# A two-layer hybrid trunk on one core: weights stored as contiguous load blocks, places of their own for the opening's loads and for the norm's outputs

## The chip, the cores and the metric

One core of one Trainium2 chip. The metric is the device time of one execution in microseconds (us). Engines go by the profile's names: PE (matmul), PEld (weight load, overlaps PE), DVE, ACT, POOL, and SP, whose queue issues most of the DMAs (SPq in rows).

## The reference, cut to what matters

512 tokens (256 context, then 256 latent) of width 1024 go through two layers; only the latent half is returned.

```python
for l in range(2):
    mod  = ada_w[l].T @ silu(c) + ada_b[l]         # six vectors of 1024, for two conditionings
    h    = x * (1 + mod.scale) + mod.shift
    p    = h @ w_in[l]                             # one projection for four mixers
    y    = concat(gdn(p), s5(p), hgrn(p), retention(p)) @ w_out[l]
    x    = layer_norm(alpha * x + mod.gate * y)
    h    = x * (1 + mod.scale2) + mod.shift2
    y    = swiglu(h, ffn_w1, ffn_w3, ffn_w2) if l == 0 else top2_of_8_experts(h, moe_w1, moe_w3, moe_w2)
    x    = layer_norm(alpha * x + mod.gate2 * y)
```

## The kernel before, in words

Activations lie feature-major: 128 features on the partitions, 512 tokens in the free dimension, eight such tiles (`KT`). A product in f32 accuracy is made of three passes in f32r: `weight` (L338) loads a raw tile by a DMA on SP's queue (L344), ACT copies it to a rounded `whi` (L348), DVE subtracts to get `wlo` (L263), and PE runs `whi` on `xh`, `whi` on `xl` and `wlo` on `xh` (L331). Most weight tiles are 512 KB (128x1024 f32) in three raw buffers `wraw`; the mixture of experts has tiles of 1 MB (128x2048) in eight buffers `mraw` (L1756).

All weights but the conditioning lie in DRAM as in the reference. A tile of `w_in`, `w_out` of layer 0 or the dense feed-forward is a strided cut: 128 rows per k-tile of 128 columns, so pieces of 512 bytes (1024 bytes where 256 columns are taken). For `moe_w1` and `moe_w3` the pieces are 2048 bytes; for `moe_w2`, `w_out` of layer 1, `ada_w` and the input `xt` a partition's piece is one whole row, 2 or 4 KB.

The order of the work (`run`, L2032):

1. `setup`, then in the pool `start` the modulation of layer 0, parts 0 and 1 (`ada`, L392): 8 loads of 512 KB each (L399) into the tag `sraw`, which has **12 buffers**, used raw by PE against the conditioning (`csk`).
2. `first_input` (L417): four 512 KB loads of `xt` (L426) into the same tag `sraw`; DVE (context half) and ACT (latent half) apply scale `sc1p` and shift, and write `xh` and `xl`.
3. `mixers(0)`: projections from `w_in`, S5 tables built on DVE and POOL (loads `s5B`, `s5C`, L1263; transposes on PE, L1278; a round trip through DRAM, `s5wt` to `s5w`), and the four mixers with their scans. A scan's input goes through DRAM too (`s5u`).
4. `mixed` (w_out, residual), `norm_feat` (L1488) with `keep` = a store of `x` to `xt1` on ACT's queue (L2045).
5. S5 tables of layer 1, `ada(1, 0)`, `ada(1, 1)`, the dense `ffn`, `ada(1, 4)`, `ada(1, 5)`, `norm_feat` again; its `keep` transposes `x` on PE (L2067), copies the result to a second tile `t` on ACT and stores `t` to `xtok` on ACT's queue (L2069).
6. `mixers(1)`, `mixed_tok` (loads `lres` from `xtok`), the mixture of experts (8 experts x 7 chunks x 6 loads of 1 MB) and the last norm.

`norm_feat`'s `m` (the modulated tile that becomes `xh`, `xl`), its `x` and the `t` of `keep` all come from `s2()` (L232): three shared buffers, in the profile `k2A`, which the mixers and the feed-forward use as well. A new tile waits until the readers of the tile three before it are done, a store among them.

The order of the instructions on each engine and each queue is fixed when the kernel is built: a list scheduler runs a model of the kernel's dependences, buffers and durations, with offsets on some functions (`prior`), and every engine and queue then works strictly in the order that it gave. A buffer more, or a load whose modelled duration changes, can therefore move instructions on every engine.

Of the kernel before, what the change touches and what calls it, by code (L numbers as in the profile page):

```python
# [143 lines left out]

def input_arrays(x):
# [14 lines left out]
    for k in ("ada_w", "w_in", "w_out", "ln_g", "ln_b", "ffn_w1", "ffn_w3", "ffn_w2", "moe_w1", "moe_w3", "moe_w2"):  # L160
        arrays[k] = np.ascontiguousarray(g(k))
# [27 lines left out]
class Trunk:  # L189
# [148 lines left out]
    def weight(self, src, shape, hi_eng="act", lo_eng="vec", pool=None, raw_bufs=3, bufs=2, tag="w", raw=None):  # L338
# [52 lines left out]
    def ada(self, l, part, pool=None, tag="w", bufs=3):  # L391
# [25 lines left out]
    def first_input(self, pool, bufs):  # L417
# [6 lines left out]
        for k0 in range(0, KT, 2):  # L424
            raw = self.t("sraw", [2, NTOK], F32, bufs, pool)
# [30 lines left out]
    def product(self, w, xh, xl, n, fn):  # L456

        for i in range(w.shape[2] // P):
            acc = self.ps("acc")[:, :n]
            self.stationary(w[:, :, i * P:(i + 1) * P], xh, xl, acc)  # L460
# [3 lines left out]
    def proj_feat(self, l, c0, fn, tok=(0, NTOK), ncol=256):  # L464

        w = self.A["w_in"][l].rearrange("(k p) f -> p k f", p=P)[:, :, c0:c0 + ncol]
        a, b = tok
        self.product(w, self.xh[:, :, a:b], self.xl[:, :, a:b], b - a, fn)

    @projecting  # L470
    def proj_tok(self, l, c0, fn, blocks, ncol=256):

        w = self.A["w_in"][l].rearrange("(k p) f -> p k f", p=P)[:, :, c0:c0 + ncol]
        blocks = list(blocks)
        accs = [self.ps("acc") for _ in range(0, len(blocks), 2)]
        for k0 in range(0, KT, 4):
            hi, lo = self.weight(w[:, k0:k0 + 4], [4, ncol], "act", "vec")
# [12 lines left out]
    def proj_few(self, l, c0, m, dst):  # L490

        w = self.A["w_in"][l].rearrange("(k p) f -> p k f", p=P)[:, :, c0:c0 + m]
        hi, lo = self.weight(w, [KT, m])
# [396 lines left out]
    def gdn_proj(self, l, full):  # L890
# [11 lines left out]
        self.proj_few(l, C_GAB, 16, self.gab)  # L902
# [586 lines left out]
    def norm_feat(self, r, pm, l, sub, part, l2, keep):  # L1489
# [28 lines left out]
        for k in range(KT):  # L1518
            x = self.s2()
# [51 lines left out]
    def mixed(self, l, src):  # L1571
# [4 lines left out]
        w = self.A["w_out"][l].rearrange("(k p) f -> p k f", p=P)  # L1576
# [13 lines left out]
    def out_part(self, l, ks, last=None):  # L1590
        w = self.A["w_out"][l].rearrange("(k p) f -> p k f", p=P)
        for k in ks:
            hi, lo = self.weight(w[:, k], [D])
# [28 lines left out]
    def ffn(self, l, xt, r):  # L1622
        A = self.A
        NF = FF // P
        w1, w3, w2 = (A[k][0].rearrange("(k p) f -> p k f", p=P) for k in ("ffn_w1", "ffn_w3", "ffn_w2"))
        gs = [[self.t(f"fg{c}{j}", [NF // 2, NTOK], F32R) for c in "hl"] for j in range(2)]
        gh, gl = ([gs[f // (NF // 2)][c][:, f % (NF // 2)] for f in range(NF)] for c in range(2))
        for f in range(NF):
            h = self.s2()
            sl = slice(f * P, f * P + P)  # L1630
            self.product(w1[:, :, sl], self.xh, self.xl, NTOK, lambda i, acc: self.silu(h, acc, self.s2()))
            self.product(w3[:, :, sl], self.xh, self.xl, NTOK, lambda i, acc: self.mul(h, h, acc))
# [120 lines left out]
    def raw_unit(self, src, n):  # L1753

        raw = self.t("mraw", [2048], F32, self.RAW, self.open["mr"][1])
        self.nc.sync.dma_start(raw.rearrange("p (a b) -> p a b", a=n), src)  # L1756
        return raw

    def unit(self, src, n, lo="vec"):
        raw = self.ahead.pop(0) if self.ahead else self.raw_unit(src, n)  # L1760
        return self.weight(src, [n, 2048 // n], "act", lo, self.mw, bufs=3, tag="m", raw=raw)

    def up_srcs(self, w1, w3, c):

        return [w[:, k0:k0 + 4, c * 512:c * 512 + 512] for w in (w1, w3) for k0 in range(0, KT, 4)]

    def up_parts(self, w1, w3, c, start=0):
        for src in self.up_srcs(w1, w3, c)[start:]:
            yield self.unit(src, 4)

    def expert(self, e):
        return [self.A[k][0].rearrange("e (k p) f -> p e k f", p=P)[:, e] for k in ("moe_w1", "moe_w3", "moe_w2")]

    def load_ahead(self):

        srcs = [src for c in range(2) for src in self.up_srcs(*self.expert(0)[:2], c)]
        self.ahead = [self.raw_unit(src, 4) for src in srcs[:self.RAW]]
# [21 lines left out]
    def down(self, w2, y, g, c):  # L1799
# [8 lines left out]
        for j0 in range(0, 4, 2):  # L1808
            hi, lo = self.unit(w2[:, 4 * c + j0:4 * c + j0 + 2, :], 2)
# [42 lines left out]
    def experts(self, jobs, first=False):  # L1852
# [5 lines left out]
        early = [self.unit(src, 4, "pool") for src in self.up_srcs(*jobs[0][:2], 0)[:3]]  # L1858
        parts = self.up_parts(*jobs[0][:2], 0, 3)
        self.ex, self.exi = [None, None], 0  # L1860
        x = {0: self.gather(jobs[0][3])}
        y, g, back = {}, {}, None
        for i in range(len(steps) + 1):
            if i < len(steps):
                n, c = steps[i]
                if i > 0:
                    parts = self.up_parts(*jobs[n][:2], c)
                g[i] = self.up(chain(early if i == 0 else (), parts), x[n])
                if c == NC - 3 and n + 1 < len(jobs):
                    x[n + 1] = self.gather(jobs[n + 1][3])  # L1870
# [5 lines left out]
            if i > 0:  # L1876
# [3 lines left out]
                self.down(jobs[n][2], y[n], g.pop(i - 1), c)  # L1880
                if c == NC - 1:
                    back = self.scatter(x[n], y[n], jobs[n][4]())
        back()

    def moe(self, l, ns):
# [17 lines left out]
        for j in range(2):  # L1903
# [8 lines left out]
        self.experts([self.expert(e) + [[self.pos[:, j, e:e + 1] for j in range(2)],  # L1912
                                               lambda e=e: [self.rG[:, j, e:e + 1] for j in range(2)]]
                      for e in range(NE)], True)
        n = nc.values_load(self.nover[0:1, 0:1], min_val=0, max_val=3)
        with self.tc.For_i(0, n, 1) as it:  # L1916
# [5 lines left out]
            dyn = [A[k][0][ds(e, 1)].rearrange("e (k p) f -> p (e k) f", p=P) for k in ("moe_w1", "moe_w3", "moe_w2")]  # L1922
# [178 lines left out]
```

## Time and profile before

| | before |
|---|---|
| three runs | 2549.09, 2555.69, 2555.76 us (median 2555.69) |
| profiled execution | 2555.49 us, its span 2553.7 us |
| PE busy | 2287.9 us, 90% |
| PEld / DVE / ACT / POOL busy | 70% / 68% / 50% / 21% |
| moved by DMA | 532.76 MB, mean 209 GB/s |
| packets under 2 KB | 169457 of 338197 |

The span runs from the first to the last instruction of the profiled execution; 1.79 us of its time lie around it. A row of a timeline gives start, duration, engine, line, operation, output<-input, and in brackets the idle time before it with what ended it. PEclk is the granted clock of PE as a share of 2.4 GHz.

### The profile page before, as it was taken

Reading aid. Unit: us, or ns where it says so; the run is one execution under the profiler, and the core shown is the slowest. Engines: PE = TensorE matmul, PEld = TensorE weight load, DVE = VectorE, ACT = ScalarE, POOL = GpSimd, SP = SyncE. Lnnn points to the kernel's source line nnn. Section 1 sums busy time; section 2 is a strip of 40 time slices with the busy share of each in tenths; the row PEclk is TensorE's granted clock in tenths of the full one; section 3 lists DMA queues with packets and bytes.
Section 4 is the critical chain, followed back from the end, with each engine's and each line's share of the span. In section 5 each row is a group of like instructions: output and inputs, shape, how many; then the busy total and the mean of one; then the engine's idle time right before and its main releaser. Section 6 shows DMA issues by size and latency. Waiting matters only on the chain. (4 is left out here: it accounts for less than half of the span.)

```text
span 2553.7 us, 33393 instructions
## 1 busy us (share of the span) xinstructions
PE 2287.9 (90%) x12928; PEld 1790.7 (70%) x12928; DVE 1737.5 (68%) x2352; ACT 1273.1 (50%) x1475; POOL 532.4 (21%) x490
## 2 busy tenths in 40 slices
PE   4979988878899999878896859999999999999997
PEld 1767756554788887447675648878787878788885
DVE  8645636778533322445646689888888888889887
ACT  1542523422544422353533337767676767676774
POOL 4423433327322200333323140000000000001000
PEclk7889987879999999888987869999999999999998
DMA  8343252415533333653230449989898989899994
GB/s 282 115 145 95 80 164 68 153 48 199 153 99 99 97 124 101 213 169 93 64 117 26 146 140 352 371 308 370 308 370 314 363 312 373 316 368 334 370 358 167
DMA packets 338197, 532.76 MB, mean 209 GB/s; under 512 B 32497, under 2 KB 169457, under 8 KB 337649
## 3 DMA queue, kind: packets, MB, share of 16 engines
q1 hardware_dynamic: 312304, 512.79, 58.4%
q10 hardware_dynamic: 25728, 17.77, 2.4%
q8 instruction: 104, 1.70, 0.3%
q14 instruction: 61, 0.49, 0.1%
HBM read 509.23 MB, written 21.28 MB: 208 GB/s over the span
## 5 line engine op out<-in xcount | busy, mean ns | idle before, releaser
L263 DVE TENSOR_TENSOR mlo<-mraw,mhi 128x2048 fp32r<-128x2048 f32 x333 | 769.9, 2325 | 110.2 <-ACT mhi L348 108.6
L348 ACT CAST mhi<-mraw 128x2048 fp32r<-128x2048 f32 x336 | 639.2, 1907 | 215.2 <-PE psh L331 134.0
L331 PE MATMUL psh<-mlo,e_xh 128*128 128x512 f32 x896 | 358.4, 400 | 6.3 <-DVE mlo L263 6.3
L331 PE MATMUL psh<-mhi,e_xh 128*128 128x512 f32 x896 | 351.9, 395 | 13.4 <-ACT mhi L348 7.8
L331 PE MATMUL psh<-mhi,e_xl 128*128 128x512 f32 x896 | 352.1, 393 | 0.0
L348 ACT CAST whi<-wraw 128x1024 fp32r<-128x1024 f32 x142 | 145.7, 1027 | 381.4 <-PE psacc L331 350.8
L331 PE MATMUL psacc<-xh,whi 128*128 128x512 f32 (+2 forms) x784 | 314.1, 402 | 23.7 <-DVE k2P L263 8.1
L263 DVE TENSOR_TENSOR wlo<-wraw,whi 128x1024 fp32r<-128x1024 f32 x142 | 179.6, 1264 | 214.9 <-ACT whi L348 212.6
L331 PE MATMUL psacc<-xh,wlo 128*128 128x512 f32 (+2 forms) x784 | 308.7, 394 | 8.8 <-DVE wlo L263 8.8
L331 PE MATMUL psacc<-xl,whi 128*128 128x512 f32 (+2 forms) x784 | 306.7, 391 | 0.0
L263 POOL TENSOR_TENSOR e_xl<-k2B,e_xh 128x512 fp32r<-128x512 f32 x16 | 31.4, 1968 | 995.9 <-ACT e_xh L1827 995.9
L331 PEld LDWEIGHTS psh<-mhi,e_xh 128*128 128x128 f32 x896 | 170.0, 190 | 52.0 <-ACT mhi L348 8.9
L331 PEld LDWEIGHTS psh<-mlo,e_xh 128*128 128x128 f32 x896 | 170.4, 190 | 43.4 <-DVE mlo L263 8.6
L331 PEld LDWEIGHTS psacc<-xh,whi 128*128 128x128 f32 (+1 forms) x784 | 152.2, 194 | 62.7 <-issue 9.5
L331 PEld LDWEIGHTS psh<-mhi,e_xl 128*128 128x128 f32 x896 | 170.2, 190 | 34.5
L331 PEld LDWEIGHTS psacc<-xh,wlo 128*128 128x128 f32 (+1 forms) x784 | 151.6, 193 | 44.6 <-DVE wlo L263 11.9
L331 PE MATMUL psy<-mlo,e_gh 128*128 128x512 f32 x448 | 176.7, 396 | 0.0
L331 PEld LDWEIGHTS psacc<-xl,whi 128*128 128x128 f32 (+1 forms) x784 | 152.0, 194 | 34.0 <-issue 4.3
L331 PE MATMUL psy<-mhi,e_gl 128*128 128x512 f32 x448 | 173.6, 391 | 0.0
L331 PE MATMUL psy<-mhi,e_gh 128*128 128x512 f32 x448 | 160.0, 394 | 0.0
L331 PEld LDWEIGHTS psy<-mhi,e_gh 128*128 128x128 f32 x448 | 84.3, 188 | 20.0 <-ACT e_gh L1806 1.5
L331 PEld LDWEIGHTS psy<-mhi,e_gl 128*128 128x128 f32 x448 | 84.2, 188 | 18.0
(532 smaller groups left out, 3778.0 us busy)
## 6 DMA issues: line engine op xcount, KB each, us to landing
mraw<-in_moe_w_dram SPq DMA_DIRECT2D x336, 1024.0 KB, 6.3
wraw<-in_ada_w_dram SPq DMA_DIRECT2D x80, 512.0 KB, 4.6
wraw<-in_ffn_w_dram SPq DMA_DIRECT2D x60, 512.0 KB, 3.9
wraw<-in_w_in_dram SPq DMA_DIRECT2D x56, 512.0 KB, 4.0
sraw<-in_ada_w_dram SPq DMA_DIRECT2D x16, 512.0 KB, 9.3
wraw<-in_w_out_dram SPq DMA_DIRECT2D x16, 512.0 KB, 3.6
s5w<-s5wt SPq DMA_DIRECT2D x8, 512.0 KB, 4.8
s5c<-s5W SPq DMA_DIRECT2D x8, 512.0 KB, 4.6
```

The source lines that it names most:

```text
L263: (eng or self.V).tensor_tensor(out=out, in0=a, in1=b, op=op)
L331: self.T.matmul(out, lhsT, rhs, start=start, stop=stop, **k)
L348: self.S.copy(hi, raw)
```

## The change

Three things.

**Layout.** On the host every weight is rearranged so that one load is one contiguous block whose partition rows follow each other: 4 KB a partition for the 512 KB loads, 8 KB for the 1 MB loads of the experts. The loads stay the same in number, size, destination and queue; only the source address pattern differs. `ada_w`, `moe_w2` and `w_out1` had whole rows per partition already, and `xt` stays as it was.

**Opening.** `sraw` has 16 buffers in place of 12, one for each `ada` load; the four `xt` loads get a tag of their own, `sx`, with four buffers. The pool grows from 48 KB to 80 KB a partition.

**Norm.** `x` of `norm_feat` gets the tag `lnx` with four buffers, the `t` of `keep` the tag `lnt` with four buffers of half the size. For the second norm a new pool `l1n` on the left side holds these and the norm's statistics; it is left just before `mixers(1)`, whose first pool on that side (`gP`, with `kq` first) then comes to lie on its place.

```diff
+FEAT_GROUPS = (0, 256, 512, C_SU, C_HQ, C_HF, C_HF + 256, C_HG, C_RQKV, C_RQKV + 256, C_RG)
+TOK_GROUPS = (C_GZ, C_HI, C_RQKV + 512)
+
+
+def weight_arrays(x):
+
+    g = lambda k: np.asarray(x[k])
+    cat = lambda *a: np.ascontiguousarray(np.concatenate([v.reshape(-1) for v in a]))
+
+    blk = lambda w, k0, kn, a, b: w[k0 * P:(k0 + kn) * P, a:b].reshape(kn, P, b - a).transpose(1, 0, 2)
+    out = {}
+    out["ada_w"] = np.ascontiguousarray(g("ada_w").reshape(DEPTH, KT, P, 6, D).transpose(0, 3, 1, 2, 4))
+    feat, tok, few = [], [], []
+    for w in g("w_in"):
+        feat.append(np.stack([blk(w, 0, KT, c + i * P, c + i * P + P).reshape(P, 1024) for c in FEAT_GROUPS for i in range(2)]))
+        tok.append(np.stack([blk(w, k0, 4, c, c + 256).reshape(P, 1024) for c in TOK_GROUPS for k0 in (0, 4)]))
+        few.append(blk(w, 0, KT, C_GAB, C_GAB + 16).reshape(P, P))
+    out["w_feat"], out["w_tok"], out["w_few"] = np.stack(feat), np.stack(tok), np.stack(few)
+    wo = g("w_out")
+    out["w_out0"] = np.stack([blk(wo[0], 0, KT, i * P, i * P + P).reshape(P, 1024) for i in range(KT)])
+    out["w_out1"] = np.ascontiguousarray(wo[1].reshape(KT, P, D))
+    for k in ("ffn_w1", "ffn_w3"):
+        out[k] = np.stack([blk(g(k)[0], 0, KT, f, f + P).reshape(P, 1024) for f in range(0, FF, P)])
+    NF = FF // P
+    out["ffn_w2"] = np.stack([cat(*(blk(g("ffn_w2")[0], k0, min(8, NF - k0), i * P, i * P + P) for k0 in range(0, NF, 8)))
+                              for i in range(KT)])
+    w1, w3, w2 = (g(k)[0] for k in ("moe_w1", "moe_w3", "moe_w2"))
+
+    moe = np.empty((NE, FE // 512, 6, P, 2048), np.float32)
+    for e in range(NE):
+        for c in range(FE // 512):
+            for j in range(2):
+                for n, w in enumerate((w1, w3)):
+                    moe[e, c, 2 * n + j] = blk(w[e], 4 * j, 4, c * 512, c * 512 + 512).reshape(P, 2048)
+                moe[e, c, 4 + j] = blk(w2[e], 4 * c + 2 * j, 2, 0, D).reshape(P, 2048)
+    out["moe_w"] = moe
+    return out
...
@@ -341,7 +383,7 @@
         v = lambda t: t if len(shape) == 1 else t.rearrange("p (a b) -> p a b", a=shape[0])
         if raw is None:
             raw = self.t(tag + "raw", [n], F32, raw_bufs, pool)
-            self.nc.sync.dma_start(v(raw), src)
+            self.nc.sync.dma_start(raw, src)
...
@@ -392,11 +434,10 @@
 
 
 
-        w = self.A["ada_w"][l].rearrange("(k p) f -> p k f", p=P)
         acc = self.ps("acc")
         for k in range(KT):
             raw = self.t(tag + "raw", [1024], F32, bufs, pool or self.wp)
-            self.nc.sync.dma_start(raw, w[:, k, part * D:(part + 1) * D])
+            self.nc.sync.dma_start(raw, self.A["ada_w"][l, part, k])
...
+    def first_input(self, pool):
 
         self.new_xm()
         xt = self.A["xt"].rearrange("(k p) t -> p k t", p=P)
@@ -422,7 +463,7 @@
         for s in range(2):
             self.ts(sc[:, s], self.mod(0, 1, s), 1.0, ALU.add)
         for k0 in range(0, KT, 2):
-            raw = self.t("sraw", [2, NTOK], F32, bufs, pool)
+            raw = self.t("sx", [2, NTOK], F32, 4, pool)
             self.nc.sync.dma_start(raw, xt[:, k0:k0 + 2])
...
-    def stationary(self, w, xh, xl, acc, eng=("act", "vec")):
-
-        K = w.shape[1]
-        for k0 in range(0, K, 8):
-            kn = min(8, K - k0)
-            hi, lo = self.weight(w[:, k0:k0 + kn], [kn, P], *eng)
+    def stationary(self, blocks, xh, xl, acc, eng=("act", "vec")):
+
+        K = sum(b.shape[1] for b in blocks) // P
+        for k0, src in zip(range(0, K, 8), blocks):
+            kn = src.shape[1] // P
+            hi, lo = self.weight(src, [kn, P], *eng)
...
+    def product(self, ws, xh, xl, n, fn):
+
+        for i, blocks in enumerate(ws):
             acc = self.ps("acc")[:, :n]
-            self.stationary(w[:, :, i * P:(i + 1) * P], xh, xl, acc)
+            self.stationary(blocks, xh, xl, acc)
             fn(i, acc)
 
     @projecting
-    def proj_feat(self, l, c0, fn, tok=(0, NTOK), ncol=256):
-
-        w = self.A["w_in"][l].rearrange("(k p) f -> p k f", p=P)[:, :, c0:c0 + ncol]
-        a, b = tok
-        self.product(w, self.xh[:, :, a:b], self.xl[:, :, a:b], b - a, fn)
+    def proj_feat(self, l, c0, fn, tok=(0, NTOK)):
+
+        g, (a, b) = FEAT_GROUPS.index(c0), tok
+        ws = [[self.A["w_feat"][l, 2 * g + i]] for i in range(2)]
+        self.product(ws, self.xh[:, :, a:b], self.xl[:, :, a:b], b - a, fn)
...
-        w = self.A["w_in"][l].rearrange("(k p) f -> p k f", p=P)[:, :, c0:c0 + ncol]
-        blocks = list(blocks)
+        g, blocks = TOK_GROUPS.index(c0), list(blocks)
         accs = [self.ps("acc") for _ in range(0, len(blocks), 2)]
         for k0 in range(0, KT, 4):
-            hi, lo = self.weight(w[:, k0:k0 + 4], [4, ncol], "act", "vec")
+            hi, lo = self.weight(self.A["w_tok"][l, 2 * g + k0 // 4], [4, ncol], "act", "vec")
...
@@ -1516,7 +1555,7 @@
                 self.act(self.xh[:, k, sl], m[:, sl], AF.Identity, bias=B)
                 self.stt(self.xl[:, k, sl], m[:, sl], B, self.xh.bitcast(F32)[:, k, sl], ALU.add, ALU.subtract)
         for k in range(KT):
-            x = self.s2()
+            x = self.t("lnx", [NTOK], bufs=4)
             self.mul(r[:, k], r[:, k], rs, eng=self.G)
             self.act(x, r[:, k], AF.Identity, scale=g[:, k:k + 1], bias=b[:, k:k + 1])
             keep(k, x)
...
-        w = self.A["w_out"][l].rearrange("(k p) f -> p k f", p=P)
+        w = [[self.A["w_out0"][i]] for i in range(KT)]
...
-            hi, lo = self.weight(w[:, k], [D])
+            hi, lo = self.weight(self.A["w_out1"][k], [D])
...
+    def raw_unit(self, src):
 
         raw = self.t("mraw", [2048], F32, self.RAW, self.open["mr"][1])
-        self.nc.sync.dma_start(raw.rearrange("p (a b) -> p a b", a=n), src)
+        self.nc.sync.dma_start(raw, src)
...
     def expert(self, e):
-        return [self.A[k][0].rearrange("e (k p) f -> p e k f", p=P)[:, e] for k in ("moe_w1", "moe_w3", "moe_w2")]
+        return lambda c, u: self.A["moe_w"][e, c, u]
...
-        start, bufs = self.enter("start", "right"), 12
+        start = self.enter("start", "right")
         for p in (0, 1):
-            self.ada(0, p, start, "s", bufs)
-        self.first_input(start, bufs)
+            self.ada(0, p, start, "s", 16)
+        self.first_input(start)
...
@@ -2055,20 +2092,20 @@
         self.enter("f0", "left")
         pm = self.ffn(0, xt1, r)
         self.leave("f0")
-        self.mx = self.open["l1"][1]
+        self.enter("l1n", "left")
         for p in (4, 5):
             self.ada(1, p)
         self.xtok = self.dr.tile([P, 2, D], F32, name="xtok")
 
         def keep(k, x):
 
-            pt, t = self.ps(), self.s2()
+            pt, t = self.ps(), self.t("lnt", [256], bufs=4)
             for j in range(2):
                 self.T.transpose(pt[:, j * P:(j + 1) * P], x[:, 256 + j * P:256 + (j + 1) * P], self.ident)
-            self.act(t[:, :256], pt[:, :256], AF.Copy)
-            self.nc.scalar.dma_start(self.xtok[:, :, k * P:(k + 1) * P], t[:, :256].rearrange("p (j x) -> p j x", j=2))
+            self.act(t, pt[:, :256], AF.Copy)
+            self.nc.scalar.dma_start(self.xtok[:, :, k * P:(k + 1) * P], t.rearrange("p (j x) -> p j x", j=2))
         self.norm_feat(r, pm, 0, 1, 0, 1, keep)
-        self.leave("l1")
+        self.leave("l1n", "l1")
```

## Rows read from the trace of the kernel before

**Rows 1.** Windows; columns as its second line names them:
```profile
core 0: us, PE busy (x) PEld busy (x) DVE busy (x) ACT busy (x) POOL busy (x), PEclk, DMA share, GB/s
16.00:20.00 4.00, 3.00 (x14) 0.43 (x12) 4.00 (x44) 0.00 (x0) 0.00 (x0) 1.00 1.03 410
140.00:150.00 10.00, 0.28 (x1) 0.00 (x0) 5.20 (x7) 4.59 (x7) 1.39 (x2) 0.72 1.09 339
640.00:960.00 320.00, 312.76 (x1356) 256.05 (x1355) 117.98 (x136) 131.13 (x186) 77.44 (x51) 0.99 0.38 113
1135.00:1165.00 30.00, 13.73 (x51) 10.16 (x52) 22.29 (x26) 8.23 (x13) 16.02 (x8) 0.66 0.23 62
2300.00:2500.00 200.00, 199.44 (x913) 163.84 (x912) 179.73 (x112) 143.53 (x98) 12.88 (x4) 1.00 0.99 355
```

**Rows 2.** Timeline of SP's queue, 0 to 130 us:
```profile
1.18 14.73 SPq L399 DMA_DIRECT2D sraw<-in_ada_w_dram  x12
16.71 0.33 SPq L1263 DMA_DIRECT2D s5B<-in_s_b_re_dram  x1
...
21.89 1.59 SPq L399 DMA_DIRECT2D sraw<-in_ada_w_dram  x2
...
26.08 0.85 SPq L399 DMA_DIRECT2D sraw<-in_ada_w_dram  x2
...
32.51 3.13 SPq L426 DMA_DIRECT2D sraw<-in_xt_dram  x4
```

**Rows 3.** Timeline of PE, 20 to 130 us:
```profile
41.66 1.11 PE L1278 MATMUL psA<-consts,s5W 128*128 128x128 f32 x4 [11.03 <-DVE s5W L263]
42.71 1.92 PE L331 MATMUL psacc<-sraw,csk 128*32 128x512 f32 x4
...
50.44 1.92 PE L331 MATMUL psacc<-sraw,csk 128*32 128x512 f32 x4
...
70.92 1.20 PE L331 MATMUL psacc<-xh,whi 128*128 128x512 f32 x2
```

**Rows 4.** Timeline of ACT, 20 to 90 us:
```profile
63.77 2.08 ACT L285 ACTIVATE sraw<-sraw,mods,sc1p 128x256 f32<-128x256 f32 x4 [9.65 <-DVE sc1p L279]
```

**Rows 5.** Waits of the engines: us in total, times, longest:
```profile
PEld psacc L331 <- DMA wraw<-in_ada_w_dram: 35.1, 21, 3.9
...
ACT whi L348 <- DMA wraw<-in_w_in_dram: 17.3, 5, 4.8
...
PE psA L331 <- DMA s5U<-s5u: 12.0, 1, 12.0
...
PE psA L2067 <- ACT k2A L285: 7.7, 3, 2.9
```

**Rows 6.** Waits of SP's queue, columns as before:
```profile
SPq L1756 <- DVE mlo L263: 850.7, 325, 14.2
```

**Rows 7.** DMA issues: count, KB each, us to landing:
```profile
lres<-xtok SPq DMA_DIRECT2D x1, 1024.0 KB, 6.0
mraw<-in_moe_w_dram SPq DMA_DIRECT2D x336, 1024.0 KB, 6.3
```

**Rows 8.** Timeline, layer 0's first norm, 666 to 671 us:
```profile
668.93 0.69 DVE L279 TENSOR_SCALAR k2A<-psacc 128x512 f32<-128x512 f32 x1 [0.52 <-DMA xt<-k2A]
...
669.68 0.50 PE L331 MATMUL psacc<-xh,whi 128*128 128x512 f32 x1 [2.31 <-DVE k2A L279]
```

**Rows 9.** Timeline, the norm behind the feed-forward:
```profile
1095.32 0.38 ACT L287 ACTIVATE k2A<-psA 128x256 f32<-128x256 f32 x1 [2.48 <-DMA xtok<-k2A]
...
1097.41 0.42 DVE L263 TENSOR_TENSOR kq<-k2P,k2P 128x256 f32<-128x256 f32 x1 [7.57 <-ACT k2P L289]
...
1100.88 0.38 ACT L287 ACTIVATE k2A<-psA 128x256 f32<-128x256 f32 x1 [0.59 <-PE psA L2067]
```

**Rows 10.** Timeline of PE, 1085 to 1175 us:
```profile
1157.83 1.06 PE L331 MATMUL psA<-s5H,s5tabwc 128*128 128x32 f32 x4 [15.38 <-DVE s5H L263]
```

More of the change, by code (lines that the diff above doesn't have):

```diff
@@ L159, in input_arrays @@
     }
-    for k in ("ada_w", "w_in", "w_out", "ln_g", "ln_b", "ffn_w1", "ffn_w3", "ffn_w2", "moe_w1", "moe_w3", "moe_w2"):
+    arrays |= weight_arrays(x)
+    for k in ("ln_g", "ln_b"):
         arrays[k] = np.ascontiguousarray(g(k))
@@ L489, in proj_few @@
     @projecting
-    def proj_few(self, l, c0, m, dst):
-        w = self.A["w_in"][l].rearrange("(k p) f -> p k f", p=P)[:, :, c0:c0 + m]
-        hi, lo = self.weight(w, [KT, m])
+    def proj_few(self, l, m, dst):
+        hi, lo = self.weight(self.A["w_few"][l], [KT, m])
         acc = self.ps("acc")
@@ L1624, in ffn @@
         NF = FF // P
-        w1, w3, w2 = (A[k][0].rearrange("(k p) f -> p k f", p=P) for k in ("ffn_w1", "ffn_w3", "ffn_w2"))
+        w2 = [[A["ffn_w2"][i, P * P * k0:P * P * (k0 + kn)].rearrange("(p f) -> p f", p=P)
+               for k0 in range(0, NF, 8) for kn in (min(8, NF - k0),)] for i in range(KT)]
         gs = [[self.t(f"fg{c}{j}", [NF // 2, NTOK], F32R) for c in "hl"] for j in range(2)]
@@ L1751, in gather, with up_srcs, up_parts @@
         return back, xh, xl
-    def raw_unit(self, src, n):
+    def raw_unit(self, src):
         raw = self.t("mraw", [2048], F32, self.RAW, self.open["mr"][1])
-        self.nc.sync.dma_start(raw.rearrange("p (a b) -> p a b", a=n), src)
+        self.nc.sync.dma_start(raw, src)
         return raw
     def unit(self, src, n, lo="vec"):
-        raw = self.ahead.pop(0) if self.ahead else self.raw_unit(src, n)
+        raw = self.ahead.pop(0) if self.ahead else self.raw_unit(src)
         return self.weight(src, [n, 2048 // n], "act", lo, self.mw, bufs=3, tag="m", raw=raw)
[L1763 to L1768, printed above, removed]
+    def up_srcs(self, w, c):
+        return [w(c, u) for u in range(4)]
+    def up_parts(self, w, c, start=0):
+        for src in self.up_srcs(w, c)[start:]:
             yield self.unit(src, 4)
     def expert(self, e):
-        return [self.A[k][0].rearrange("e (k p) f -> p e k f", p=P)[:, e] for k in ("moe_w1", "moe_w3", "moe_w2")]
+        return lambda c, u: self.A["moe_w"][e, c, u]
     def load_ahead(self):
-        srcs = [src for c in range(2) for src in self.up_srcs(*self.expert(0)[:2], c)]
-        self.ahead = [self.raw_unit(src, 4) for src in srcs[:self.RAW]]
+        srcs = [src for c in range(2) for src in self.up_srcs(self.expert(0), c)]
+        self.ahead = [self.raw_unit(src) for src in srcs[:self.RAW]]
     def up(self, parts, x):
@@ L1856, in experts @@
         steps = [(n, c) for n in range(len(jobs)) for c in range(NC)]
-        early = [self.unit(src, 4, "pool") for src in self.up_srcs(*jobs[0][:2], 0)[:3]]
-        parts = self.up_parts(*jobs[0][:2], 0, 3)
+        early = [self.unit(src, 4, "pool") for src in self.up_srcs(jobs[0][0], 0)[:3]]
+        parts = self.up_parts(jobs[0][0], 0, 3)
         self.ex, self.exi = [None, None], 0
-        x = {0: self.gather(jobs[0][3])}
+        x = {0: self.gather(jobs[0][1])}
         y, g, back = {}, {}, None
@@ L1879, in experts @@
                     y[n] = [self.ps(f"y{h}") for h in range(2)]
-                self.down(jobs[n][2], y[n], g.pop(i - 1), c)
+                self.down(jobs[n][0], y[n], g.pop(i - 1), c)
                 if c == NC - 1:
-                    back = self.scatter(x[n], y[n], jobs[n][4]())
+                    back = self.scatter(x[n], y[n], jobs[n][2]())
         back()
@@ L1911, in moe @@
         self.enter("m", "left")
-        self.experts([self.expert(e) + [[self.pos[:, j, e:e + 1] for j in range(2)],
-                                               lambda e=e: [self.rG[:, j, e:e + 1] for j in range(2)]]
-                      for e in range(NE)], True)
+        self.experts([(self.expert(e), [self.pos[:, j, e:e + 1] for j in range(2)],
+                       lambda e=e: [self.rG[:, j, e:e + 1] for j in range(2)]) for e in range(NE)], True)
         n = nc.values_load(self.nover[0:1, 0:1], min_val=0, max_val=3)
@@ L1921, in moe @@
             e = nc.values_load(ei[0:1, 0:1], min_val=0, max_val=NE - 1, engines=[mybir.EngineType.SP])
-            dyn = [A[k][0][ds(e, 1)].rearrange("e (k p) f -> p (e k) f", p=P) for k in ("moe_w1", "moe_w3", "moe_w2")]
-            self.experts([dyn + [[ov[:, j:j + 1] for j in (0, 1)], lambda: [ov[:, j:j + 1] for j in (2, 3)]]])
+            dyn = lambda c, u: A["moe_w"][ds(e, 1), c, u].rearrange("e p f -> p (e f)")
+            self.experts([(dyn, [ov[:, j:j + 1] for j in (0, 1)], lambda: [ov[:, j:j + 1] for j in (2, 3)])])
         self.leave("m")
```

19 lines of the change are left out of this document (7 added, 12 removed).

## The prediction

> **What bounds the kernel now.** I read the windows first, to see which engine each stage hangs on. The experts keep PE busy 199.44 of 200 us at the full clock, and the feed-forward 312.76 of 320 [rows 1]. DVE is 180 of 200 us busy beside it, and the DMA engines are full (355 GB/s), but neither is waited for: SP's queue stands 850.7 us, 325 times, because an expert load has no free buffer yet [rows 6], and among the engines' waits there is none for `mraw`. In these two stages PE is at work throughout, and nothing in this change takes a matmul away.
>
> What is left are the holes. Three bear on the change. In the opening PE does no projection before 70.92 us [rows 3]. In the mixers PE stands 12.0 us once for an S5 input that goes through DRAM [rows 5]; the window 140 to 150 us is that hole (PE 0.28 of 10 us, clock 0.72) [rows 1]. Round the two norms PE waits for ACT or DVE tiles that have no free buffer [rows 5, 8, 9].
>
> The sum is made against the profiled execution: span 2553.7 us, its time 2555.49 us, so 1.79 us lie around the span, and that time stands 0.2 us under the median of the three runs, 2555.69. Anything under 0.3%, some 7.7 us, I count as no change.
>
> **Layout of the experts and the feed-forward: 0.** A 1 MB expert load lands 6.3 us after issue in pieces of 2 and 4 KB; the one load of that size whose partitions' rows are 8 KB in one piece, as the new blocks' are, `lres`, took 6.0 [rows 7]. Even 0.3 us on each of 336 loads would end in a longer wait for a buffer, since 850.7 us of such waits stand ahead of them [rows 6]. The cover is PE at 99.7%; were it gone, the price would be those 336 x 0.3 = 101 us, but a landing is not waited for. The feed-forward's 60 loads stand behind the same cover at 113 GB/s and a DMA share of 0.38 [rows 1].
>
> **Layout of `w_in`: -2 us.** In the opening, with rows of 4 KB, the engines moved 410 GB/s at a share of 1.03; in the feed-forward, with 512-byte pieces, 113 at 0.38 [rows 1]. At full share that is 398 against 297 GB/s. A 512 KB load costs 524288 B / 297 = 1.77 us in short pieces and 1.32 in long ones, so 0.45 us less. It is felt where ACT waits for `w_in`: five waits, 17.3 us [rows 5], so 5 x 0.45 = 2.2 us. Bounds: 0 (other transfers fill the engines) to -17.3/4 = -4.3, since 0.45 is a quarter of 1.77. I take -2, nearest to the row.
>
> The trace shows shorter pieces moving less per busy engine. The Trainium skill, DMA: Bandwidth & Descriptors, section Specifications, sets the smallest transfer at line rate at 512 B; by it this term would be 0 and the sum 2 us smaller. No run here shows it yet.
>
> **Opening: -18 us.** Today SP issues twelve `ada` loads at once at 1.18 us, then S5's loads from 16.71; the last four `ada` loads wait for a free `sraw` buffer and go out by two at 21.89 and 26.08, and `xt` only at 32.51 [rows 2]. The matmuls on those loads got a late place in PE's fixed order: behind transposes that wait 11.03 us for DVE's S5 tables, so they run at 42.71 and 50.44 [rows 3]. `sc1p` needs the last of them, and ACT starts modulating at 63.77 after 9.65 us of idling [rows 4]: 11.4 us after the last `ada` matmul, which ends at 52.36. The first projection follows 7.15 us later, at 70.92.
>
> With 16 + 4 buffers nothing holds the 20 loads back. At 410 GB/s [rows 1] the 16 of `ada`, 8.39 MB, take 20.5 us and `xt` 5.1 more, so from 1.18 on the `ada` loads would be in by 22 and, with S5's loads of 16.71 to 26 in the same engines, by some 31; `xt` by 36. The last `ada` matmul then ends near 32. If DVE's S5 work delays `sc1p` as today, modulation starts 11.4 us later, at 43, and projection 7.15 behind that, at 50.5; if not, `xt` sets it, at 36 and 43. That is 20 to 28 us earlier than 70.92. No instruction is added; 20 issues are moved ahead of S5's loads on SP's queue.
>
> How much reaches the end? What is late next is S5's own chain. Its tables are built on DVE and POOL meanwhile and gain nothing; the wait for `s5U`, 12.0 us [rows 5], ends at the same time as before if the tables set it, and then eats up to 12.0 of the gain. So the term lies between 20 - 12 = 8 and 28. I take 18, the middle, for part of that chain starts from the projection itself.
>
> **Norm of layer 0: -2.3 us.** `x` is stored from a shared buffer, and DVE's tile behind it waits for that store; PE stands 2.31 us for the DVE tile [rows 8]. With four `lnx` buffers the mixers' and the feed-forward's tiles no longer queue behind the store. Bounds 0 to -2.3; I take the row.
>
> **Norm of the feed-forward: -5 us.** `x` and `t` alternate in three buffers, so each round waits for a store: PE waited 7.7 us in three times for ACT's `x` [rows 5], ACT 2.48 before a copy [rows 9]. With eight private buffers these go: at most 7.7 + 2.48 = 10.2 us. But PE stands 15.38 us later for the states of S5 [rows 10] in a window where DVE is 22.29 of 30 us busy [rows 1], a chain that these buffers touch only in part. Bounds -10.2 to 0; I take the middle. The new pool adds one wait: `gP`, first `kq` at 1097.41, now lies on the statistics and `x`, and may wait until the norm's last ACT copy at 1100.88 [rows 9], at worst +3.5 us on a DVE that had idled 7.57 before; I take 0, for `kq` feeds a chain behind which other projections run.
>
> **Sum.** -2 - 18 - 2.3 - 5 = -27.3. 2553.7 - 27.3 = 2526.4, with 1.79 around it 2528.2: **2528 us**.
>
> **Rivals.**
> *The gain is absorbed.* PE's order is made anew by the scheduler; if S5 tables and not projections set the first mixer's end, the 20 to 28 us come back as longer waits before `s5U` and the gdn scan. For it speaks that PE idles at 140 us with its projections done; against it that the wait there is 12.0 and not 28. Then the opening gives 28 - 12.0 x 2 = 4 (the wait there, and as much in the scan behind it), the norms 7.3: 2555.5 - 4 - 7.3 = 2544. This is also the time if the `ada` matmuls keep their late places, and the change so doesn't do in the order what it does in the buffers.
>
> *Contiguous blocks land sooner.* PE waits 35.1 us, 21 times, for modulation weights in `wraw` [rows 5]. They have 4 KB rows already, so I count nothing; the Trainium skill, Perfetto Trace Analysis, section Contiguity and DMAs, says the same (contiguity only matters within one partition's line), and no row tests it. If blocks that lie in one piece are read faster by the quarter found above, 8.8 us go, and with the full 28 of the opening the time is 2555.5 - 28 - 2 - 2.3 - 5 - 8.8 = 2509.
>
> *Slower: S5's loads behind the bulk.* Its place is SP's queue and the 16 engines in the first 36 us. `s5B` went out at 16.71 [rows 2] while the engines were full [rows 1]; behind 20 bulk loads it would land not at some 20 but at 36, some 17 us later. DVE builds the tables from it, and is the engine that PE waits for (11.03 us) [rows 3]; the tables, the gdn chain and the first scan then end up to 17 us later, and the projections moved up only fill PE's wait. The price is +17 less the 7.3 of the norms: 2555.5 + 17 - 7.3 = 2565. It decides if the S5 tables and not PE's projections set the first mixer's end by more than the 12.0 us of [rows 5]. Against it: SP's slots for `s5B` follow free buffers, and the scheduler may put them between the bulk loads.
>
> **Chances and range.** Forecast 0.60, absorbed 0.18, sooner 0.12, slower 0.10. The forecast's case runs from 2513 (28, 10.2, 2.3 and 2.2 all gained) to 2547 (8 of the opening alone). For 8 in 10 the range takes in both the absorbed case up to no change, 2556, and the sooner case with its 2509 and the 17.3 of `w_in` bound to ACT, 2492; what is left out is the slower case and stray ends. Faster by over 0.3% (under 2548): 0.60 + 0.12 and a half of 0.18, less 0.03 for the forecast's tail, so 0.78. Within 0.3%: the other half, the tail and a little of the slower case, 0.13. Slower: 0.09.
>
> **What would show it.** Right: SP's first run counts 16 `ada` loads and 4 of `xt` by some 20 us; the last `ada` matmul ends by 32 us and the first projection starts by 51; the hole at 140 us is shorter or earlier; no tile waits for a store to `xt` or `xtok`; PE's waits for ACT at the transposes are gone; expert loads still wait for DVE, and PE's share of the experts' window stays above 0.99. Wrong: a first projection after 60 us, an S5 wait of over 20 us, a wait of PE for `mraw`, or `ada` waits of the second layer that fall by a quarter or more.

## The result and the profile after

The changed kernel takes 2570.74 us, the median of 20 runs, beside 2551.1 for 20 runs of the kernel before: a ratio of **1.0059, interval 1.0036 to 1.0081**, so 15 us slower (9 to 21). The ratio leaves out the slowest execution, 2586.5 us, which counts as slow; the medians of all runs lie 19.6 us apart. The runs can be split in two groups, 5 from 2546.0 to 2555.7 and 15 from 2560.6 to 2586.5. The gap between them is only 5 us, but the granted clock, averaged over an execution, parts them too: 0.923 to 0.928 in the first group, 0.908 to 0.921 in the second. The runs of the kernel before lie between 2540.7 and 2559.8. The profiled execution, 2571.95 us with a span of 2570.1, belongs to the upper group.

First the windows of the changed kernel, columns as in [rows 1].

```profile
core 0: us, PE busy (x) PEld busy (x) DVE busy (x) ACT busy (x) POOL busy (x), PEclk, DMA share, GB/s
140.00:150.00 10.00, 10.00 (x45) 6.66 (x46) 3.16 (x4) 6.94 (x20) 5.35 (x4) 1.00 0.42 152
230.00:270.00 40.00, 40.00 (x135) 28.12 (x134) 4.15 (x6) 1.31 (x4) 0.44 (x3) 0.50 0.15 46
2300.00:2500.00 200.00, 199.44 (x912) 163.84 (x911) 179.71 (x114) 143.56 (x99) 13.02 (x4) 1.00 0.94 352
```

The experts are as before: PE 199.44 of 200 us, and from their first matmul to the end 1038.5 us in place of 1038.9. The hole at 140 us is filled (0.28 us of work before). But from 230 to 270 us PE is busy without a break at **half its clock**, 1.2 GHz. The kernel before is as busy in this stretch, at 1.00:

```profile
230.00:270.00 40.00, 40.00 (x168) 27.52 (x167) 24.77 (x35) 18.84 (x29) 13.77 (x17) 1.00 0.39 103
```

SP's queue, to be held against [rows 2]:

```profile
1.19 16.56 SPq L440 DMA_DIRECT2D sraw<-in_ada_w_dram  x16
18.70 4.21 SPq L467 DMA_DIRECT2D sx<-in_xt_dram  x4
23.82 18.05 SPq L386 DMA_DIRECT2D wraw<-in_w_feat_dram  x5
41.91 0.42 SPq L1302 DMA_DIRECT2D s5B<-in_s_b_re_dram  x1
...
156.31 0.79 SPq L1353 DMA_DIRECT2D s5t<-s5wt  x2
```

All 20 bulk loads go out at once, as forecast, and `s5B` follows at 41.91 in place of 16.71. On PE, against [rows 3]:

```profile
27.69 1.05 PE L373 MATMUL psacc<-sraw,csk 128*32 128x512 f32 x4 [0.24 <-DMA sraw<-in_ada_w_dram]
...
39.17 0.80 PE L373 MATMUL psacc<-xh,whi 128*128 128x512 f32 x1 [8.67 <-ACT whi L390]
...
174.91 0.64 PE L373 MATMUL psA<-s5U,s5tabwc 128*128 128x64 f32 x4
```

The last `ada` matmul ends at 28.7 us, not 52.4, and the first projection starts at 39.17, not 70.92. But S5's first product on `s5U`, at 152.3 us before, starts at 174.91. DVE tells why:

```profile
20.29 0.17 DVE L305 TENSOR_TENSOR mods<-psP,params 128x16 f32<-128x16 f32 x1 [8.88 <-PE psP L373]
30.53 0.17 DVE L305 TENSOR_TENSOR mods<-psP,params 128x16 f32<-128x16 f32 x1 [10.07 <-PE psP L373]
...
41.42 1.29 DVE L305 TENSOR_TENSOR xl<-sx,xh 128x512 fp32r<-128x512 f32 x2
42.63 0.17 DVE L305 TENSOR_TENSOR s5st<-exp,exi 128x16 f32<-128x16 f32 x1
```

DVE stands idle 8.88 and 10.07 us for the modulation, and `s5st`, the first instruction of the S5 tables behind their constants, runs at 42.63, right behind the opening's last `xl`. In the kernel before it ran at 8.80, and the tables' last load (`s5t`) went out at 133.51, here at 156.31. These two rows of the kernel before, of DVE and of SP's queue:

```profile
8.80 0.17 DVE L263 TENSOR_TENSOR s5st<-exp,exi 128x16 f32<-128x16 f32 x1
```
```profile
133.51 1.06 SPq L1314 DMA_DIRECT2D s5t<-s5wt  x2
```

`s5st` carries no wait in the compiled changed kernel; the scheduler put it there. The places in the two compiled kernels show the only new tie. The S5 tables' pool `tab` lies at 123264 to 171008 bytes of a partition in both. The opening's pool `start` lay at 180192 to 229344 and now begins at 147424: **it reaches 23 KB onto the tables' place**. Theory A was therefore that the loss comes from the opening's pool lying there, not from the loads; rivals were the blocks (B), the norm's pool (C), S5's loads behind the bulk on SP's queue (A2), and a new order that costs by itself (D).

How far the delay reaches is seen at two later places of PE, the first product of `w_out` and the experts' first matmul. Before, these are

```profile
544.62 1.22 PE L331 MATMUL psacc<-xh,whi 128*128 128x512 f32 x2 [3.10 <-ACT xh L824]
...
1514.80 0.79 PE L331 MATMUL psh<-mhi,e_xh 128*128 128x512 f32 x1 [5.64 <-ACT e_xh L1749]
```

and in the changed kernel `w_out` starts at 574.84, 30 us late, and the experts at 1531.63, 17 us late. The loss arises in the first mixers, and part of it is won back behind them.

The engines' waits and then the DMA issues of the changed kernel, against [rows 5] and [rows 7]:

```profile
PEld psacc L373 <- DMA wraw<-in_ada_w_dram: 34.5, 21, 4.0
...
ACT whi L390 <- DMA wraw<-in_w_feat_dram: 14.8, 4, 8.4
...
PEld psA L2104 <- ACT lnx L327: 4.8, 3, 4.0
...
PEld psA L373 <- DMA s5U<-s5u: 3.3, 1, 3.3
```
```profile
lres<-xtok SPq DMA_DIRECT2D x1, 1024.0 KB, 5.6
...
mraw<-in_moe_w_dram SPq DMA_DIRECT2D x336, 1024.0 KB, 5.8
```

PE's own wait for ACT's `x` at the transposes falls from 7.7 us in three times to 3.1 us in one, and for `s5U` PEld waits 3.3 us where PE stood 12.0. An expert load lands in 5.8 us in place of 6.3, and nothing waits for it; with the layout alone it lands in 6.6, so the layout is not what the difference shows.

### The profile page after: what moved, and what is told of

Read it like the earlier page. It is cut to its first block, busy times and chain, and to the rows that moved or that the text cites. A ratio compares the mean times of both kernels' runs of the same rounds, so it can differ in the third digit from the quotient of the medians.

```text
span 2570.1 us, 33386 instructions
## 1 busy us (share of the span) xinstructions
PE 2311.4 (90%) x12928; PEld 1805.7 (70%) x12928; DVE 1746.5 (68%) x2352; ACT 1271.0 (49%) x1475; POOL 527.1 (21%) x490
## 5 line engine op out<-in xcount | busy, mean ns | idle before, releaser
L373 PE MATMUL psacc<-xh,wlo 128*128 128x512 f32 (+2 forms) x784 | 314.5, 401 | 17.8 <-DVE wlo L305 17.7
```

The lines of the kernel that those rows point to most:

```text
L373: self.T.matmul(out, lhsT, rhs, start=start, stop=stop, **k)
```

## The experiments

Each ratio stands against runs of the kernel before that were taken beside it.

**One part at a time.** The layout leaves the order on every engine and queue as it was, instruction for instruction, so it can be taken by itself.

*Layout alone*: the changed kernel with

```diff
-        start = self.enter("start", "right")
+        start, bufs = self.enter("start", "right"), 12
...
-            raw = self.t("sx", [2, NTOK], F32, 4, pool)
+            raw = self.t("sraw", [2, NTOK], F32, bufs, pool)
...
-            x = self.t("lnx", [NTOK], bufs=4)
+            x = self.s2()
...
-            pt, t = self.ps(), self.t("lnt", [256], bufs=4)
+            pt, t = self.ps(), self.s2()
```

and `l1n` not entered.

> Only the contiguous blocks; the order of the instructions on every engine and queue is the one of before. Theory A (the loss comes from the opening's larger pool, which reaches onto the place of the S5 tables and lets their work start only when the opening is over): about 2549 us beside 2551, ratio 0.996 to 1.000, the five waits of ACT for w_in shorter, 15 us or less in place of 17.3. Rival B (the blocks themselves cost time): ratio 1.003 or more, and longer landings. An experts' load lands in 5.8 us in place of 6.3 in either case, and that is worth nothing.

Measured: 2549.55 beside 2556.84 us, ratio 0.997 (0.9959 to 0.9981). B (the blocks themselves cost time) falls; the gain is 7.7 us.

*Opening alone*, on the kernel before:

```diff
-            raw = self.t("sraw", [2, NTOK], F32, bufs, pool)
+            raw = self.t("sx", [2, NTOK], F32, 4, pool)
...
-            self.ada(0, p, start, "s", bufs)
+            self.ada(0, p, start, "s", 16)
```

> Only the 16 + 4 buffers of the opening, the weights as before. Theory A: the whole loss is here, ratio 1.005 to 1.012 (2564 to 2582 us beside 2551); the first S5 table instruction on DVE behind the last xl of the opening, at 40 us or later, and the wait of SP's queue for S5's inputs 15 to 25 us longer than before. Rival C (the norm's buffers bring the loss): ratio 0.988 to 0.996, since the projections start near 39 us in place of 71.

Measured: 2580.35 beside 2556.84, ratio **1.0109** (1.0075 to 1.0142), in two groups: three runs from 2565.8 to 2569.8, three from 2590.9 to 2592.8. By the ratio it costs 28 us (by the medians 23.5). The whole loss is here.

*Norm alone*, on the kernel before:

```diff
-            x = self.s2()
+            x = self.t("lnx", [NTOK], bufs=4)
...
-        self.mx = self.open["l1"][1]
+        self.enter("l1n", "left")
...
-            pt, t = self.ps(), self.s2()
+            pt, t = self.ps(), self.t("lnt", [256], bufs=4)
...
-        self.leave("l1")
+        self.leave("l1n", "l1")
```

> Only the norm's own buffers and the pool l1n. Theory A: ratio 0.996 to 1.000 (0 to 10 us gained), PE's wait for ACT at the transposes of the second norm gone. Rival C: ratio 1.003 or more, with the first kq of layer 1 waiting for the norm's last copy.

Measured: 2546.17, ratio 0.9964 (0.9951 to 0.9976), 9 us gained. C (the norm's pool) falls. PE's wait at the transposes is not quite gone, 3.1 us are left.

*Layout and norm*: the changed kernel with the opening of before.

```diff
-            self.ada(0, p, start, "s", 16)
+            self.ada(0, p, start, "s", bufs)
...
-            raw = self.t("sx", [2, NTOK], F32, 4, pool)
+            raw = self.t("sraw", [2, NTOK], F32, bufs, pool)
```

> The changed kernel with the opening of before: 12 shared buffers. Theory A: ratio 0.994 to 0.999, faster than before by 2 to 14 us, and some 15 to 30 us faster than the changed kernel. If the parts don't add up (the order is made anew with each of them) the ratio is at 1.003 or more.

Measured: 2541.22, ratio **0.9937** (0.9921 to 0.9952): 16 us faster than the kernel before, a little more than theory A allowed, and the fastest of all. The parts add up: 1.0109 x 0.9937 = 1.0045, inside the changed kernel's interval.

**The pool's place.** *14 and 15 places*: the opening alone, with fewer `ada` places.

```diff
-            self.ada(0, p, start, "s", 16)
+            self.ada(0, p, start, "s", 10)
```

(and 11 in the second). With four `xt` places these are 56 KB, 1 KB clear of the tables, and 60 KB, 3 KB onto them.

> The opening alone, on the kernel before, with 10 + 4 places (56 KB) in place of 16 + 4: the pool ends 1 KB short of the S5 tables' place. SP's queue still sends 10 ada and 4 xt loads ahead of the first s5B. Theory A1 (what costs is that the pool lies on the tables' place, so that their work is put behind the opening): first S5 table instruction on DVE before 6 us, ratio 0.992 to 1.003. Rival A2 (what costs is that S5's loads go behind the bulk on SP's queue, wherever the pool lies): ratio 1.005 or more.

> The same with one more ada place, 11 + 4 (60 KB): the pool now reaches 3 KB onto the place of the tables' last tile. A1: the first S5 table instruction on DVE at 40 us or later, ratio 1.005 to 1.014 as with 16 + 4, so 15 to 30 us above the run with 14 places. A2, or a cost that grows with the number of loads sent ahead: at most a fifth of that between 14 and 15 places, 5 us or less.

Measured: 1.0081 (1.0057 to 1.0104) with 14 and 1.0165 (1.0138 to 1.0192) with 15. SP's queue of both, 14 first:

```profile
19.45 0.34 SPq L1263 DMA_DIRECT2D s5B<-in_s_b_re_dram  x1
...
130.69 0.81 SPq L1314 DMA_DIRECT2D s5t<-s5wt  x2
```
```profile
35.47 3.13 SPq L1263 DMA_DIRECT2D s5B<-in_s_b_re_dram  x1
...
161.89 0.93 SPq L1314 DMA_DIRECT2D s5t<-s5wt  x2
```

One place more moves the end of the tables from 130.69 to 161.89: that the tables are late comes from the place. With 14 places S5's loads stand behind 14 bulk loads as well, and the tables end 3 us earlier than in the kernel before, so the delay that A2 names is not there. But its ratio, 1.005 or more, is, and A1 missed with 0.992 to 1.003: the tables are in time and the kernel is still 21 us slower. With 15 places the loss is above A1's range. And the 21 us between the two are not all the tables': the profile with 15 places has PE at half clock around 230 to 275 us, that with 14 has not.

*All loads early, clear of the tables*: the changed kernel with

```diff
-        start = self.enter("start", "right")
+        start, left = self.enter("start", "right"), self.enter("startl", "left")
...
-            self.ada(0, p, start, "s", 16)
+            self.ada(0, p, start, "s", 13)
...
-            raw = self.t("sx", [2, NTOK], F32, 4, pool)
+            raw = self.t("sx", [2, NTOK], F32, *((1, pool) if k0 == 6 else (3, left)))
```

> The changed kernel (layout and norm kept), but the opening's tiles beside the tables: 13 ada places and one xt place on the right, three xt places on the left where gP comes later. A1: S5's table work on DVE starts before 6 us, modulation between 30 and 45 us, ratio 0.980 to 0.994, at least as fast as layout and norm without the opening (0.9937), and up to 12 us faster. If the projections of the first layer are not what sets the end of its mixers, it stays at 0.992 to 0.996. A2: ratio 1.000 or more.

Measured: 2547.46 beside 2557.94, ratio 0.9967 (0.9948 to 0.9985); SP's first load for S5, then PE's rows:

```profile
25.76 0.33 SPq L1302 DMA_DIRECT2D s5B<-in_s_b_re_dram  x1
```
```profile
56.50 1.22 PE L373 MATMUL psacc<-xh,whi 128*128 128x512 f32 x2 [5.12 <-ACT xh L476]
...
144.11 3.65 PE L373 MATMUL psA<-s5U,s5tabwc 128*128 128x64 f32 x16 [4.22 <-DMA s5tabwc<-s5w]
```

S5's products start 8 us earlier than in the kernel before and the projections 14, though 19 of the 20 bulk loads go ahead of `s5B`: A2 falls. Beside the changed kernel (1.0059) that is 0.92 points, some 23 us. The place was moved, but 13 `ada` loads go out at once in place of 16, the order is another, and PE's clock is 1.00 from 230 to 270 us, so the 23 us hold the fall of the clock as well. A1 had said 0.980 to 0.994, and this too is a miss: beside layout and norm with the opening of before (0.9937) it wins nothing. By the traces it is 5 us ahead at w_out's first product (536.02 and 541.22) and 6 us behind at the experts' first matmul (1510.4 and 1504.2), since the order of layer 1 came out differently too.

*The place without the loads*: the kernel before with an unused tile in the opening's pool.

```diff
+        self.G.memset(self.t("pad", [3072], F32, 1, start)[:, :8], 0.0)
```

> The kernel before with its 12 shared buffers and an unused tile of 12 KB in the opening's pool, which now reaches 3 KB onto the S5 tables' place (with a tile of 8 KB, 56 KB in all, it doesn't, and the order of PE, DVE, ACT and SP is the one of before, instruction for instruction). No load gains a place. Theory A1 (lying on the tables' place is what costs): first S5 table instruction on DVE behind the opening, at 35 us or later; S5's first product 15 to 30 us later than the 152 us of before; ratio 1.004 to 1.020. Rival D (any new order costs, the hold itself nothing, because the projections go ahead meanwhile): S5 late as well, but ratio 0.997 to 1.003.

Measured: 2575.75 beside 2554.81, ratio **1.0073** (1.0048 to 1.0099), 19 us. A row of DVE, then its PE rows:

```profile
46.34 0.17 DVE L263 TENSOR_TENSOR s5st<-exp,exi 128x16 f32<-128x16 f32 x1
```
```profile
39.89 1.22 PE L331 MATMUL psacc<-xh,whi 128*128 128x512 f32 x2 [3.16 <-ACT xh L435]
...
174.18 3.68 PE L331 MATMUL psA<-s5U,s5tabwc 128*128 128x64 f32 x32
```

No load gained a place, and the first projection is at 39.89 all the same, S5's first product at 174.18: both as in the changed kernel. So no place was needed to bring the projections forward: the tables went out of DVE's way. By its trace w_out's first product is 6 us late (551.01), the experts' first matmul 20 (1534.64). PE's clock is 1.00 from 230 to 270 us, so this loss is not the fall of the clock seen there in the changed kernel.

*One place more, clear of the tables*, on the kernel before:

```diff
-        start, bufs = self.enter("start", "right"), 12
+        start, bufs = self.enter("start", "right"), 13
```

> The kernel before with 13 shared buffers in place of 12 (52 KB, clear of the tables): one load more goes out early, a change that by the trace is worth at most 2 us. A1 and a well-behaved order: ratio 0.997 to 1.003. Rival D (the scheduler's order for everything behind it is made anew, and such an order is worth 10 to 20 us either way): ratio outside 0.996 to 1.004, with the opening itself as before.

Measured: 1.0039 (1.0018 to 1.006), 10 us slower for one load that goes out earlier. S5's first product comes 5 us earlier than in the kernel before and the first expert matmul 5 us later, in another order in between. Neither condition on record is met: 1.0039 lies between A1's 1.003 and D's 1.004, and the opening is not as before (the first projection starts at 62.69). But the interval excludes 1, so an order made anew can cost some 10 us with the tables in time, as 14 places cost 21. A part of D stands beside A.

**The clock.** The opening alone once more, for a profile of the other group:

> One more look at the 16 + 4 opening alone, whose runs stand in two groups, 2566 to 2570 and 2591 to 2593 us. Theory E (the groups are PE's clock: in the slower one it falls at the short waits near 225 us and stays at 1.2 GHz for some 50 us of full work): a time of 2588 or more goes with a granted clock near 0.5 from 230 to 270 us, one of 2572 or less with 1.00 there. Otherwise (the groups come from elsewhere, such as DMA): the clock of that stretch doesn't go with the time.

Measured: 2596.94 us, one execution. Windows of the first profiled execution (2565.8 us), then of this one, of the same program:

```profile
200.00:220.00 20.00, 18.58 (x95) 14.06 (x94) 18.12 (x18) 7.59 (x12) 10.89 (x6) 0.99 0.21 52
220.00:225.00 5.00, 4.96 (x18) 3.63 (x18) 4.89 (x5) 0.18 (x2) 0.51 (x1) 0.68 0.39 105
225.00:230.00 5.00, 4.36 (x25) 3.13 (x26) 3.49 (x5) 2.23 (x4) 2.53 (x2) 1.00 0.40 108
230.00:270.00 40.00, 36.60 (x190) 27.14 (x190) 17.71 (x24) 13.44 (x23) 7.04 (x7) 0.97 0.42 112
```
```profile
200.00:220.00 20.00, 19.86 (x108) 15.39 (x106) 17.67 (x19) 6.16 (x11) 11.17 (x6) 1.00 0.21 53
220.00:225.00 5.00, 3.01 (x12) 2.17 (x12) 4.95 (x4) 1.90 (x3) 2.12 (x2) 1.00 0.38 105
225.00:230.00 5.00, 4.04 (x13) 2.38 (x14) 4.62 (x6) 2.40 (x4) 0.77 (x1) 0.68 0.18 36
230.00:270.00 40.00, 40.00 (x133) 28.09 (x134) 4.15 (x6) 0.66 (x2) 1.90 (x4) 0.50 0.18 55
```

Up to 220 us the clock is alike, 0.99 and 1.00. About then PE stops for DVE, in the first execution

```profile
219.42 0.52 PE L331 MATMUL psacc<-xh,wlo 128*128 128x512 f32 x1 [1.42 <-DVE wlo L263]
...
226.65 0.65 PE L331 MATMUL psP<-ra,rv 128*64 128x256 f32 x2 [0.64 <-DVE ra L263]
```

and in the second

```profile
221.30 0.50 PE L331 MATMUL psacc<-xh,wlo 128*128 128x512 f32 x1 [1.44 <-DVE wlo L263]
...
225.96 0.66 PE L331 MATMUL psA<-s5H,s5tabwc 128*128 128x64 f32 x4 [1.64 <-DVE s5H L263]
```

In the first the clock falls for under 5 us (0.68 over 220 to 225) and comes back. In the second it falls between 225 and 230 and stays at 0.50 through 40 us in which PE never pauses. S5's last product ends at 307 us in place of 283, w_out starts 24 us later, and the run ends 31 us later. PE's order is the same in the changed kernel up to the norm of layer 0, and its profile shows the same fall: 0.50 goes with the upper groups in these three profiles and 0.97 with the lower. Theory E holds for them. A profile of the changed kernel's lower group was not taken.

The first execution also shows where the opening loses time without this fall. Its rows for `w_out` and the experts:

```profile
555.39 1.22 PE L331 MATMUL psacc<-xh,whi 128*128 128x512 f32 x2 [3.10 <-ACT xh L824]
...
1525.28 0.79 PE L331 MATMUL psh<-mhi,e_xh 128*128 128x512 f32 x1 [6.99 <-ACT e_xh L1749]
```

It is 10.8 us late at the first and 10.5 at the second: all of it is lost by the end of the first mixers.

**The layout.** *Only the `ada` blocks*, on the kernel before, with the `ada_w` line of the change's `weight_arrays` and

```diff
-            self.nc.sync.dma_start(raw, w[:, k, part * D:(part + 1) * D])
+            self.nc.sync.dma_start(raw, self.A["ada_w"][l, part, k])
```

> Only ada_w as contiguous blocks of 512 KB; its rows of 4 KB per partition are as long as before, and the order is that of before. If only the length of a partition's row counts: ratio 0.999 to 1.001 and PE's wait for ada loads still 35 us. If a block in one piece lands sooner: that wait near 25 us as with all weights laid out, ratio 0.996 to 0.998.

*All but the `ada` blocks*: layout alone with that line undone.

> The counterpart: every weight but ada_w as contiguous blocks, 4 KB rows in place of 512 bytes for w_in, w_out and the feed-forward, and the order of before. If the layout's gain is all in the ada blocks: ratio 0.9985 to 1.0015, PE's wait for ada loads near 35 us, ACT's for w_in 13 to 17. If the longer rows bring it too (they free the engines on which the ada loads wait): ratio 0.996 to 0.998 and both waits shorter, 25 to 30 us and 10 to 14.

Measured: 0.9971 (0.995 to 0.9992) and 0.9986 (0.997 to 1.0002). The waits with layout alone, only `ada`, and all but `ada`:

```profile
PEld psacc L373 <- DMA wraw<-in_ada_w_dram: 25.0, 17, 3.1
...
ACT whi L390 <- DMA wraw<-in_w_feat_dram: 13.4, 5, 3.3
```
```profile
PEld psacc L332 <- DMA wraw<-in_ada_w_dram: 28.1, 19, 3.7
...
ACT whi L349 <- DMA wraw<-in_w_in_dram: 15.8, 5, 4.1
```
```profile
PEld psacc L374 <- DMA wraw<-in_ada_w_dram: 32.2, 21, 3.8
...
ACT whi L391 <- DMA wraw<-in_w_feat_dram: 15.6, 5, 4.3
```

Against 35.1 and 17.3 us before, PE's wait for `ada` falls to 28.1 when only its blocks change and to 32.2 when only the others do. The `ada` blocks carry the gain that can be measured; for the rest the interval holds no change. The two intervals overlap, and each wait is that of one execution: norm alone, in an order of its own and with the `ada` rows of before, shows 28.0 as well:

```profile
PEld psacc L331 <- DMA wraw<-in_ada_w_dram: 28.0, 20, 3.0
```

The landings are steadier. An `ada` load into `wraw` lands in 4.3 to 4.5 us (median of a trace) in the five traces with blocks and in 4.5 to 4.7 in the nine without.

## Why the prediction was wrong

- **Layout of the experts and the feed-forward, 0:** right as far as the runs show, for nothing waits for these loads. The feed-forward's land in 3.4 to 3.5 us in place of 3.9; the experts' show no such step (6.3 before, 5.8 to 6.6 with blocks).
- **Layout of `w_in`, -2:** its own size was near: without the `ada` blocks ACT's five waits fall by 1.7 us, from 17.3 to 15.6. But the layout gained 7.7 us (5 to 10), and for another reason. The term held that loads with rows of 4 KB stay as they are. Their rows do, but an `ada` load in one piece landed in 4.3 us in place of 4.6, among the loads on which PE waits 21 times. The mechanism is, by these runs, that of the rival "contiguous blocks land sooner"; its price of 8.8 us was near. The Trainium skill, Perfetto Trace Analysis, section Contiguity and DMAs, says that contiguity only matters within a partition's line. The ratio of 0.9971 (0.995 to 0.9992) with unchanged lines speaks against it here. The Trainium skill, DMA: Bandwidth & Descriptors, section Specifications, sets the smallest transfer at line rate at 512 B. On that the runs don't decide: feed-forward loads land in 3.9 us with pieces of 512 bytes and in 3.4 to 3.5 with rows of 4 KB, but these rows also lie in one piece, which alone brought the `ada` loads 0.3 us; and in the kernel's time, without `ada`, the interval reaches 1.0002.
- **Opening, -18:** the failed step. Its loads did what was written, more so (projection at 39, not 43 to 50.5). "Its tables are built on DVE and POOL meanwhile and gain nothing" is what failed: they lost 23 us, and the projections' lead was lost behind them. I had costed the places as buffers in a queue and never looked where 80 KB lie. And the lead is not worth what the term took even with the tables in time: in the opening laid clear of them the projections are 14 us earlier than with the opening of before, w_out's first product 5, the end not at all. One sentence of the term was wrong in its cause, too: a place more does bring the projections forward (62.69 with 13), but no place was needed, because DVE had the tables first; with the tables held and the 12 buffers of before they start at 39.89.
- **Norms, -7.3:** right, 9 us (6 to 13); how it divides between the two norms no run shows. The wait that `gP` was to add shows in no total.
- **The slower rival** had the right sign and the right victim, but its place was wrong: SP's queue. With the opening clear of the tables 19 bulk loads stand ahead of `s5B` and the tables are in time. That its price (2565) came near is luck, since it held nothing of the clock.
- **What no term held:** the clock. With the opening alone the middles of the two groups, 2569.0 and 2591.9, lie 23 us apart; in the changed kernel 2552.4 and 2572.0, so 20, with 15 of 20 runs in the upper. Of the opening's loss of 28 us (by the ratio, over both groups) its lower group shows 12. The changed kernel's lower group lies 1 us above the kernel before: there layout and norms pay for the opening, and by the groups, an estimate, its loss of 15 us is the fall of the clock. The Trainium skill, TensorE: Matmul & The Clock Gate, Part 1, says that activity releases the throttle. The second execution shows it kept through 40 us of unbroken work.
- **The signs.** Of those that were to show the forecast right nearly all came: 20 loads in SP's first run, the last `ada` matmul at 28.7, the first projection at 39.17, the hole at 140 us filled, no tile waiting for a store, PE's share of the experts' window at 0.997; only of the wait at the transposes 3.1 us were left. Of those that were to show it wrong one came: PEld's waits for the second layer's `ada` weights, those from 570 us on (600 in the changed kernel), fell from 24.4 to 14.9 us. Norm alone, without blocks, has 16.6 there, so it does not point to the blocks alone. No sign asked when the S5 tables end, and that is where the delay began.

What stays open: how much of those 12 us is the late S5 chain itself and how much the other order. The tile that only takes the place has the tables 22 us late and w_out 6 us late, and costs 19 us in all; 14 places have the tables in time and w_out 8 us late (552.87), and cost 21. So it is shown that the place makes the tables late, and that a pool on that place can cost 19 us with no buffer added for any load, but not that the late tables are what costs it. Telling them apart needs an order held fixed, which wasn't tried. Nor was it tried to take the short stops near 225 us away, so the rows show only that they stand ahead of the fall of the clock.

## What to carry to other kernels

A buffer's price includes its place: before giving an opening more room, look at what the allocator lays under it, for a scheduler may hold a whole pool of early work back for 3 KB of overlap. Change one part at a time when a scheduler remakes the order, since a change that is worth nothing by its own waits came out at 10 us here; data layout left the order alone here, so its runs could be compared without that scatter. A gain at the start counts only as far as the chain that ends the stage starts from it.

## What was not expected of the hardware

One program ran at two speeds, 2565.8 and 2596.9 us, by PE's clock: after stops of some 1.5 us it stayed at 1.2 GHz over 40 us of unbroken work in one execution and came back within 5 us in the other. Loads of 512 KB with rows of 4 KB landed in 4.3 us as one piece of DRAM and in 4.6 as rows 24 KB apart, in the same order of work (0.9971, 0.995 to 0.9992). And the feed-forward's loads of the same size landed in 3.9 us in pieces of 512 bytes in nine traces, and in 3.4 to 3.5 as one piece with rows of 4 KB in five.
